# Average pooling, 2x2: one more whole store queued behind the last loads, and the last tile in two pieces instead of four

## The chip, the cores and the metric

The kernel runs on one core of one Trainium2 chip. The metric is the time of one execution on the device in microseconds (us).

## The reference

```python
# x: (32, 128, 256, 256) float32, kernel_size = 2, stride = 2; output (32, 128, 128, 128) float32
window = x[:, :, 2*i : 2*i + 2, 2*j : 2*j + 2]
output[:, :, i, j] = np.mean(window, axis=(2, 3))
```

The input is 1073.7 MB and the output 268.4 MB. Every byte is moved once.

## The kernel before

The rows of the image are taken in pairs. A unit is 128 row pairs, one on each partition: 2 KB of input and 512 B of output per partition. There are 4096 units: 127 whole tiles of 32 units (numbers 0 to 126) and a last tile of 32 units that goes in pieces. A whole tile is a load of 8.39 MB (64 KB per partition) and a store of 2.10 MB (16 KB per partition).

There are two input buffers (`ins`) and three result buffers (`res`). Whole tiles alternate between buffers 0 and 1; the last tile has `res[2]`. SP (SyncE) issues the loads, DVE (VectorE) makes the sums (rows, then neighbours), ACT (ScalarE) multiplies by 0.25 and issues the stores. A load or store is a DMA: the issuing engine puts it on its queue and goes on, 16 DMA engines move it, and it has landed when it has added 16 to its semaphore. In the code, `take(engine, sem, n)` makes an engine wait until a semaphore holds n, and takes n off it.

```python
    whole, rest = divmod(units - 1, TILE)      # 127, and rest + 1 = 32
    rest += 1
    parts, a = [], 0
    while a < rest:                            # pieces of 16, 8, 4, 4 units
        b = rest if rest - a <= 4 else a + (rest - a) // 2
        parts.append((a, b, sem(f"part{len(parts)}")))
        a = b
    # ... cut: load(), scale() ...
    def sums(it, dst):
        dve.tensor_add(out=it[:, :, 0:w], in0=it[:, :, 0:w], in1=it[:, :, w:]).then_inc(halfway)
        take(dve, halfway)
        dve.tensor_add(out=dst, in0=it[:, :, 0:w:2], in1=it[:, :, 1:w:2]).then_inc(summed)

    def tile_sums(b):
        take(dve, stored[b], 16)               # the result buffer must be free again
        take(dve, loaded[b], 16)
        sums(ins[b], res[b])

    def scale_store(t, b, landed):
        take(act, summed)
        act.sem_inc(free[b])
        scale(res[b])
        take(act, scaled)
        act.dma_start(out=ot[t], in_=res[b]).then_inc(landed, 16)
    # ... cut: SP loads tiles 0 to 126 as input buffers come free ...
        take(sp, free[whole % 2])
        it, dst = ins[whole % 2], res[2]
        for a, b, part in parts:               # loads of the last tile
            sp.dma_start(out=it[:, a:b], in_=block((whole * TILE + a) * P, b - a)[0]).then_inc(part, 16)
        take(sp, held)                         # tile 126 scaled: its store goes on SP's queue
        sp.dma_start(out=ot[whole - 1], in_=res[(whole - 1) % 2]).then_inc(tail, 16)
    # ... cut: DVE sums tiles 0 to 126, then the pieces; ACT scales and stores tiles 0 to 124 ...
        for t in range(1 + 2 * pairs, whole - 1):      # only t = 125
            scale_store(t, t % 2, stored[t % 2] if t < whole - 2 else tail)
        take(act, summed)
        scale(res[(whole - 1) % 2], held)
        for a, b, _ in parts:
            take(act, summed)
            scale(dst[:, a:b])
            take(act, scaled)
            act.dma_start(out=block((whole * TILE + a) * P, b - a)[1], in_=dst[:, a:b]).then_inc(tail, 16)
```

Of the kernel before, what the change touches and what calls it, by code (L numbers as in the profile page):

```python
# [9 lines left out]
@with_exitstack  # L10
def kernel(
    ctx: ExitStack,
    tc: tile.TileContext,
    x: bass.AP,
    kernel_size: bass.AP,
    stride: bass.AP,
    out: bass.AP,
):
    nc = tc.nc
    P = nc.NUM_PARTITIONS  # L20

    n, c, h, w = x.shape
    k = int(kernel_size)
    s = int(stride)
    h_out = (h - k) // s + 1
    w_out = (w - k) // s + 1
    R = n * c * h_out
    units = R // P if R % P == 0 else 0


    if k == 2 and s == 2 and h % 2 == 0 and w == 256 and units >= 1024:
        _pool_2x2(ctx, tc, x, out, units)
    else:
        _generic_pool(ctx, tc, x, out, k, s, n, c, h, w, h_out, w_out)
# [5 lines left out]
def _pool_2x2(ctx, tc, x, out, units):  # L40
    nc = tc.nc
    P = nc.NUM_PARTITIONS
    f32 = mybir.dt.float32
    w = x.shape[3]
    w_out = w // 2
    sp, act, dve = nc.sync, nc.scalar, nc.vector

    xv = x.rearrange("n c (ho a) w -> (n c ho) (a w)", a=2)
    ov = out.rearrange("n c ho wo -> (n c ho) wo")


    in_pool = ctx.enter_context(tc.tile_pool(name="inp", bufs=2))
    out_pool = ctx.enter_context(tc.tile_pool(name="outp", bufs=3))
    ins = [in_pool.tile([P, TILE, 2 * w], f32, name="in_tile") for _ in range(2)]
    res = [out_pool.tile([P, TILE, w_out], f32, name="res") for _ in range(3)]

    def sem(name):
        return ctx.enter_context(nc.semaphore(name))

    loaded, free, stored = [[sem(f"{n}{b}") for b in range(2)] for n in ("loaded", "free", "stored")]  # L60
    halfway, summed, scaled, held, tail = [sem(n) for n in ("halfway", "summed", "scaled", "held", "tail")]



    def take(engine, sem, n=1):
        engine.wait_ge(sem, n)
        engine.sem_inc(sem, -n)  # L67

    def block(r0, g):
        rows = slice(r0, r0 + g * P)  # L70
        return xv[rows].rearrange("(p g) f -> p g f", p=P), ov[rows].rearrange("(p g) f -> p g f", p=P)

    whole, rest = divmod(units - 1, TILE)
    rest += 1
    xt = xv[0:whole * TILE * P].rearrange("(t p g) f -> t p g f", p=P, g=TILE)
    ot = ov[0:whole * TILE * P].rearrange("(t p g) f -> t p g f", p=P, g=TILE)
    parts, a = [], 0
    while a < rest:
        b = rest if rest - a <= 4 else a + (rest - a) // 2
        parts.append((a, b, sem(f"part{len(parts)}")))  # L80
        a = b

    def load(t, b):
        sp.dma_start(out=ins[b], in_=xt[t]).then_inc(loaded[b], 16)
# [7 lines that stand above are left out]
        take(dve, stored[b], 16)  # L92
        take(dve, loaded[b], 16)
        sums(ins[b], res[b])

    def scale(dst, done=scaled):
        act.mul(out=dst, in_=dst, mul=0.25).then_inc(done)  # L97
# [8 lines that stand above are left out]
    with tc.tile_critical():  # L106

        load(0, 0)
        load(1, 1)
        pairs = (whole - 2) // 2  # L110
        with sp.Fori(2, 2 + 2 * pairs, 2) as i:
            for b in range(2):
                take(sp, free[b])
                load(i + b, b)
        for t in range(2 + 2 * pairs, whole):
            take(sp, free[t % 2])
            load(t, t % 2)



        take(sp, free[whole % 2])
        it, dst = ins[whole % 2], res[2]
        for a, b, part in parts:
            sp.dma_start(out=it[:, a:b], in_=block((whole * TILE + a) * P, b - a)[0]).then_inc(part, 16)
        take(sp, held)
        sp.dma_start(out=ot[whole - 1], in_=res[(whole - 1) % 2]).then_inc(tail, 16)


        for b in range(2):
            dve.sem_inc(stored[b], 16)  # L130
        with dve.Fori(0, whole // 2):
            for b in range(2):
                tile_sums(b)
        if whole % 2:
            tile_sums(0)
        for a, b, part in parts:
            take(dve, part, 16)
            sums(it[:, a:b], dst[:, a:b])


        scale_store(0, 0, stored[0])
        pairs = (whole - 3) // 2
        with act.Fori(1, 1 + 2 * pairs, 2) as i:
            for b in (1, 0):
                scale_store(i + 1 - b, b, stored[b])
        for t in range(1 + 2 * pairs, whole - 1):
            scale_store(t, t % 2, stored[t % 2] if t < whole - 2 else tail)
        take(act, summed)
        scale(res[(whole - 1) % 2], held)
        for a, b, _ in parts:  # L150
            take(act, summed)
            scale(dst[:, a:b])
            take(act, scaled)
            act.dma_start(out=block((whole * TILE + a) * P, b - a)[1], in_=dst[:, a:b]).then_inc(tail, 16)


        take(sp, tail, 16 * (len(parts) + 2))
# [95 lines left out]
```

## Time and profile before

| | before |
|---|---|
| median of 3 runs | 3103.59 us (3103.52 to 3103.79) |
| profiled span | 3101.5 us |
| moved by DMA | 1342.19 MB at a mean of 433 GB/s |
| DVE, ACT busy | 54%, 15% |

The head of the page of before: busy time by engine (us, share of the span), then the span in 40 slices, where a digit is tenths of busy time.

```profile
DVE 1679.6 (54%) x262; ACT 464.7 (15%) x132; POOL 0.2 (0%) x4
...
DMA  9999999999999999999999999999999999999999
...
DMA packets 37728, 1342.19 MB, mean 433 GB/s; under 512 B 4192, under 2 KB 4192, under 8 KB 4576
```

The DMA is full from end to end and neither compute engine is near its limit, so the kernel is bound by its bytes. The Trainium skill, "DMA: Bandwidth & Descriptors", section Where 436 GB/s comes from, puts the ceiling of the fabric on the side of SBUF, the on-chip memory, at 435 GB/s. The trace agrees: from 500 to 1500 us it moved 434 GB/s. (The same section expects transfers between HBM, the main memory, and SBUF, as these are, to be bound by HBM at about 358 GB/s; the measurement decides.) Only the first and last microseconds can be made better.

The tail is therefore what matters. The timeline of before: start, duration, engine, line, operation, and in brackets the idle time ahead of it.

```profile
3033.88 0.34 SPq L84 DMA_DIRECT2D in_tile<-in_x_dram  x1
3037.71 0.34 ACTq L104 DMA_DIRECT2D out_dram<-res  x1
...
3058.06 1.84 SPq L124 DMA_DIRECT2D in_tile<-in_x_dram  x4
3061.76 0.35 ACTq L104 DMA_DIRECT2D out_dram<-res  x1
3067.57 8.69 DVE L87 TENSOR_TENSOR in_tile<-in_tile 128x8192 f32<-128x8192 f32 x1 [9.71 <-DVEq L67]
3076.41 4.43 DVE L89 TENSOR_TENSOR res<-in_tile 128x4096 f32<-128x4096 f32 x1
3080.75 4.42 DVE L87 TENSOR_TENSOR in_tile<-in_tile 128x4096 f32<-128x4096 f32 x1
...
3084.66 0.35 SPq L126 DMA_DIRECT2D out_dram<-res  x1
...
3094.44 0.69 DVE L89 TENSOR_TENSOR res<-in_tile 128x512 f32<-128x512 f32 x1
3095.25 0.63 ACT L97 ACTIVATE res<-res 128x512 f32<-128x512 f32 x1 [1.34 <-ACTq L67]
3095.98 0.34 ACTq L154 DMA_DIRECT2D out_dram<-res  x1
```

The lines are, in order: the load of tile 126, the store of tile 124, the four loads of the last tile, the store of tile 125 (here on the ACT queue), the sums of tile 126, the first sum of the last tile, the store of tile 126, and the end of the last piece. DVE works from 3067.57 to 3095.13 without a gap worth naming.

The trace also gives the time from issue to landing. The load of tile 126 took 31.6 us (landed 3065.5). The store of tile 124 took 29.6 us (landed 3067.3), just before DVE started. The store of tile 125 took 19.5 us (landed 3081.3), and the last store, of 0.26 MB, 4.4 us (landed 3100.4). The line of the last store, with its size and the time to landing:

```profile
out_dram<-res ACTq DMA_DIRECT2D x1, 256.0 KB, 4.4
```

The fine windows of before: stretch, its length, busy time of DVE, ACT and POOL, clock, share of the 16 DMA engines, GB/s. A packet, the piece in which a DMA engine moves data, counts in full in the stretch in which it starts, so a share can exceed 1.

```profile
3098.50:3098.75 0.25, 0.00 (x0) 0.00 (x0) 0.00 (x0) 1.00 1.00 385
3098.75:3099.00 0.25, 0.00 (x0) 0.00 (x0) 0.00 (x0) 1.00 0.38 139
3099.00:3099.25 0.25, 0.00 (x0) 0.00 (x0) 0.00 (x0) 1.00 0.11 41
...
3099.75:3100.00 0.25, 0.00 (x0) 0.00 (x0) 0.00 (x0) 1.00 0.04 16
3100.00:3100.25 0.25, 0.00 (x0) 0.00 (x0) 0.00 (x0) 1.00 0.00 0
```

The DMA is full until about 3098.8.

### The profile page before, as it was taken

To read this page: it belongs to the slowest core of one execution; us is meant where nothing else is said; L and a number is where in the kernel's file an instruction comes from. 1 tells how busy PE (TensorE), PEld (TensorE's weight loads), DVE (VectorE), ACT (ScalarE), POOL (GpSimd) and SP (SyncE) were. 2 spreads that over 40 slices of the span, in tenths; PEclk is the share of its full clock that TensorE was granted. 3 is DMA by queue.
4 is the path that set the end of the run, shared out by engine and by line. 5 is a ranking of instruction groups with operands and counts; after the bars stand their busy time and mean duration, and the time that the engine had idled before them with its cause. 6 is when DMAs were issued, how large, how long until landed. Compare 5 with 4: busy or idle time off the path is not lost. (4 is left out here: it accounts for less than half of the span.)

```text
span 3101.5 us, 2614 instructions
## 1 busy us (share of the span) xinstructions
DVE 1679.6 (54%) x262; ACT 464.7 (15%) x132; POOL 0.2 (0%) x4
## 2 busy tenths in 40 slices
DVE  4555555555555555555555555555555555555556
ACT  1111111111111111111111111111111111111111
POOL 0000000000000000000000000000000000000000
DMA  9999999999999999999999999999999999999999
GB/s 416 436 440 426 436 440 426 437 440 424 438 440 423 439 437 425 440 428 434 440 433 430 442 423 436 439 427 440 435 426 437 439 427 436 438 424 439 437 425 416
DMA packets 37728, 1342.19 MB, mean 433 GB/s; under 512 B 4192, under 2 KB 4192, under 8 KB 4576
## 3 DMA queue, kind: packets, MB, share of 16 engines
q1 hardware_dynamic: 19008, 1075.85, 80.1%
q10 hardware_dynamic: 18720, 266.35, 20.1%
HBM read 1073.74 MB, written 268.44 MB: 433 GB/s over the span
## 5 line engine op out<-in xcount | busy, mean ns | idle before, releaser
L87 DVE TENSOR_TENSOR in_tile<-in_tile 128x8192 f32<-128x8192 f32 (+1 forms) x131 | 1113.0, 8496 | 1396.4 <-DVEq L67 1396.4
L97 ACT ACTIVATE res<-res 128x4096 f32<-128x4096 f32 (+1 forms) x131 | 463.5, 3538 | 2594.8 <-ACTq L67 2594.8
L89 DVE TENSOR_TENSOR res<-in_tile 128x4096 f32<-128x4096 f32 (+1 forms) x131 | 566.8, 4327 | 19.2
L97 ACT ACT_TABLE_LOAD x1 | 1.3, 1283 | 36.3 <-ACTq L67 36.3
L234 POOL MEMSET const-bfloat16-1.0<- 128x1 bf16 x1 | 0.1, 101 | 0.0
L234 POOL MEMSET const-uint8-127<- 128x1 uint8 x1 | 0.1, 101 | 0.0
L234 POOL MEMSET const-float32-0.0<- 128x1 f32 x1 | 0.1, 98 | 0.2 <-issue 0.2
L234 POOL MEMSET const-float32-1.0<- 128x1 f32 x1 | 0.1, 98 | 0.0
## 6 DMA issues: line engine op xcount, KB each, us to landing
out_dram<-res ACTq DMA_DIRECT2D x126, 2048.0 KB, 30.8
in_tile<-in_x_dram SPq DMA_DIRECT2D x1, 4096.0 KB, 22.0
in_tile<-in_x_dram SPq DMA_DIRECT2D x1, 2048.0 KB, 27.1
in_tile<-in_x_dram SPq DMA_DIRECT2D x2, 1024.0 KB, 30.0
out_dram<-res SPq DMA_DIRECT2D x1, 2048.0 KB, 11.7
in_tile<-in_x_dram SPq DMA_DIRECT2D x127, 31.5
out_dram<-res ACTq DMA_DIRECT2D x1, 1024.0 KB, 8.1
out_dram<-res ACTq DMA_DIRECT2D x1, 512.0 KB, 6.0
```

The lines of the kernel that those rows point to most:

```text
L87: dve.tensor_add(out=it[:, :, 0:w], in0=it[:, :, 0:w], in1=it[:, :, w:]).then_inc(halfway)
L89: dve.tensor_add(out=dst, in0=it[:, :, 0:w:2], in1=it[:, :, 1:w:2]).then_inc(summed)
L97: act.mul(out=dst, in_=dst, mul=0.25).then_inc(done)
L234: nc = _bacc.Bacc("TRN2", target_bir_lowering=False, num_devices=1)
```

## The change

Its intent is to let the last loads pass first, since sums and stores hang on them, and to fill the DMA afterwards with stores that are ready. The store of tile 125 moves from the ACT queue to the SP queue, where it stands behind the last loads, as the store of tile 126 already did. The last tile goes in two halves of 16 units instead of pieces of 16, 8, 4 and 4.

```diff
-        b = rest if rest - a <= 4 else a + (rest - a) // 2
+        b = rest if a else (rest + 1) // 2
 # ... cut: the semaphore held becomes held[0], held[1] ...
-        take(sp, held)
-        sp.dma_start(out=ot[whole - 1], in_=res[(whole - 1) % 2]).then_inc(tail, 16)
+        for k, t in enumerate((whole - 2, whole - 1)):
+            take(sp, held[k])
+            sp.dma_start(out=ot[t], in_=res[t % 2]).then_inc(tail, 16)
 # ... cut ...
-        for t in range(1 + 2 * pairs, whole - 1):
-            scale_store(t, t % 2, stored[t % 2] if t < whole - 2 else tail)
-        take(act, summed)
-        scale(res[(whole - 1) % 2], held)
+        for t in range(1 + 2 * pairs, whole - 2):
+            scale_store(t, t % 2, stored[t % 2])
+        for k, t in enumerate((whole - 2, whole - 1)):
+            take(act, summed)
+            if k == 0:
+                act.sem_inc(free[t % 2])
+            scale(res[t % 2], held[k])
```

More of the change, by code (lines that the diff above doesn't have):

```diff
@@ L60, in _pool_2x2 @@
     loaded, free, stored = [[sem(f"{n}{b}") for b in range(2)] for n in ("loaded", "free", "stored")]
-    halfway, summed, scaled, held, tail = [sem(n) for n in ("halfway", "summed", "scaled", "held", "tail")]
+    halfway, summed, scaled, tail = [sem(n) for n in ("halfway", "summed", "scaled", "tail")]
+    held = [sem(f"held{k}") for k in range(2)]
     def take(engine, sem, n=1):
```

## The prediction

> **What bounds the kernel now.** The DMA engines. The page's head gives a span of 3101.5 us in which 1342.2 MB move at a mean of 433 GB/s; the slices show DMA at 9 tenths everywhere; DVE is 54%, ACT 15% busy. The Trainium skill ("DMA: Bandwidth & Descriptors", Where 436 GB/s comes from) puts the ceiling at 435 GB/s; the trace agrees: loads alone at the start (second tile's sums begin 19.3 us after the first's, for 8.39 MB) run at 434 GB/s, like the mixture in the middle. Only the ends are elastic. In fine windows DMA is full until about 3098.9; the last store lands at 3100.4 (issued 3095.98, 4.4 us to landing).
>
> **The tail before, from the timeline.** DVE starts tile 126 at 3067.57, when the store of tile 124 (issued 3037.71, 29.6 us) lands, not when its load does (3033.88 + 31.6 = 3065.5). From there DVE works almost gapless to 3095.13: whole tile to 3080.84, the half of 16 units 3080.75 to 3087.61, then 8, 4 and 4 units. The part loads land at 3080.1, 3085.6, about 3088.1 and 3090; the store of tile 125 competes with them and lands at 3081.3.
>
> **What the change does.** No byte is added or removed. The 2.10 MB store of tile 125 moves from the ACT queue, where it shares engines with the last loads, to the SP queue behind them (the skill, same page, Queues, rings and completion order: a ring is consumed in order, engines round-robin between rings). Estimate: 2.10 MB / 434 GB/s = 4.8 us, so the last load lands near 3085.4 instead of 3090. The last tile goes in 2 pieces instead of 4.
>
> **On the critical path.** The earlier loads are worth almost nothing: DVE is occupied with tile 126 until 3080.8 and the first half until 3087.6 in both versions, and the second half is there by then. The end changes. Second half: DVE 3087.53 + 4.42 + 0.15 + 2.29 = 3094.4 (0.7 us earlier than now); ACT 1.91 us instead of 0.63, so the last store is issued at about 3096.5 instead of 3096.0; and it is 1.05 MB instead of 0.26. After 3096.5 only 0.98 MB moved before, so the DMA must run out of other stores first: a gap of about 0.2 us plus 0.6 us from issue to first byte. Then 1.05 MB / 434 = 2.4 us: data end near 3099.5 to 3099.9, landing near 3101.2. Net: **+0.8 us**.
>
> **Predicted time: 3104.4 us, 8 in 10 between 3102.6 and 3106.8.** Chances: faster by over 2%: 0.003; within 2%: 0.994; slower by over 2%: 0.003. A tail change cannot move 62 us.
>
> **What would show each step.** (a) The two part loads land near 3076 and 3085 us. (b) Sums of tile 126 still start near 3067.6, the chain of DVE stays gapless, ends near 3094.4. (c) The stores of tiles 125 and 126 on the SP queue land near 3090 and 3096. (d) The last store is issued near 3096.5 and takes 4.5 to 5 us to land; fine windows show a DMA dip around 3096 to 3097.5. (e) Middle unchanged, about 434 GB/s.
>
> **What would make it wrong.** If the SP queue with two stores behind loads drains less evenly over the 16 engines, the tail grows by a few us. If the deferred stores leave the DMA with backlog at 3096.5, the last store shares with them and ends 1 us later still. A drift of 0.1% in the middle is 3 us and hides everything.

## The result, and the profile after

| | before | after |
|---|---|---|
| median of 6 runs each | 3103.60 us (3103.26 to 3103.79) | 3103.68 us (3102.89 to 3104.79) |
| ratio of the fast runs | | 1.0001, 95% interval 0.9988 to 1.0014 |
| profiled span | 3101.5 us | 3101.1 us |

The interval is about 4 us to either side. A difference in the tail of less than that has to be read from the traces.

For that I count from one event that the change does not touch: the issue of the load of tile 126, at 3033.88 us in before and 3033.53 us in after. The 0.35 us between the two arose earlier in the run and is not the change's.

The timeline of after, for the same stretch; its line numbers are a few higher.

```profile
3033.53 0.34 SPq L85 DMA_DIRECT2D in_tile<-in_x_dram  x1
3037.38 0.34 ACTq L105 DMA_DIRECT2D out_dram<-res  x1
...
3057.73 0.86 SPq L125 DMA_DIRECT2D in_tile<-in_x_dram  x2
3061.42 23.25 SPq L128 DMA_DIRECT2D out_dram<-res  x2
3067.23 8.69 DVE L88 TENSOR_TENSOR in_tile<-in_tile 128x8192 f32<-128x8192 f32 x1 [9.71 <-DVEq L68]
3076.07 4.42 DVE L90 TENSOR_TENSOR res<-in_tile 128x4096 f32<-128x4096 f32 x1
3080.42 4.42 DVE L88 TENSOR_TENSOR in_tile<-in_tile 128x4096 f32<-128x4096 f32 x1
...
3087.19 4.42 DVE L88 TENSOR_TENSOR in_tile<-in_tile 128x4096 f32<-128x4096 f32 x1
...
3091.76 2.29 DVE L90 TENSOR_TENSOR res<-in_tile 128x2048 f32<-128x2048 f32 x1
3094.17 1.91 ACT L98 ACTIVATE res<-res 128x2048 f32<-128x2048 f32 x1 [4.86 <-ACTq L68]
3096.19 0.35 ACTq L159 DMA_DIRECT2D out_dram<-res  x1
```

The two halves landed 17.8 and 27.1 us after their issue, at about 3075.5 and 3085.2 us. In before the last three loads had landed at 3085.6 and later, up to about 3090.5. So the loads did come earlier, as intended. DVE took no notice: it started tile 126 at the same distance from the reference event (33.70 us in after, 33.69 us in before), again had no gap, and took up the second half at 3087.19, two microseconds after that half had landed.

The fine windows of after, in the columns used above.

```profile
3096.00:3096.25 0.25, 0.00 (x0) 0.08 (x1) 0.00 (x0) 1.00 1.08 459
3096.25:3096.50 0.25, 0.00 (x0) 0.00 (x0) 0.00 (x0) 1.00 0.40 164
3096.50:3096.75 0.25, 0.00 (x0) 0.00 (x0) 0.00 (x0) 1.00 0.09 33
3096.75:3097.00 0.25, 0.00 (x0) 0.00 (x0) 0.00 (x0) 1.00 0.00 0
3097.00:3097.25 0.25, 0.00 (x0) 0.00 (x0) 0.00 (x0) 1.00 1.26 524
...
3099.25:3099.50 0.25, 0.00 (x0) 0.00 (x0) 0.00 (x0) 1.00 1.26 524
3099.50:3099.75 0.25, 0.00 (x0) 0.00 (x0) 0.00 (x0) 1.00 0.04 0
```

There is now a hole between 3096.25 and 3097.00. The stores that were held back are done, and the last store (1.05 MB) has just been issued at 3096.19. The idle shares add up to 0.60 + 0.91 + 1.00 quarters, 0.63 us. But the end is sharp: the last packets end within 0.14 us of each other, the last at 3099.70, where in before one or two engines trailed for a microsecond. The last store landed 3.9 us after its issue, at 3100.1:

```profile
out_dram<-res ACTq DMA_DIRECT2D x1, 1024.0 KB, 3.9
```

Counted from the reference event that is 66.5 us, as in before. The last store was issued 0.56 us later than in before (62.66 us after the reference event against 62.10) and took 0.57 us less to land (3.86 against 4.43, from the landing times that the traces keep). That the two cancel is an accident of the sizes.

### The profile page after: what moved, and what is told of

Read it like the earlier page. It is cut to its first block, busy times and chain, and to the rows that moved or that the text cites. A ratio compares the mean times of both kernels' runs of the same rounds, so it can differ in the third digit from the quotient of the medians.

```text
span 3101.1 us, 2596 instructions
## 1 busy us (share of the span) xinstructions
DVE 1679.2 (54%) x258; ACT 464.5 (15%) x130; POOL 0.2 (0%) x4
## 5 line engine op out<-in xcount | busy, mean ns | idle before, releaser
L88 DVE TENSOR_TENSOR in_tile<-in_tile 128x8192 f32<-128x8192 f32 x129 | 1112.8, 8626 | 1396.0 <-DVEq L68 1396.0
L98 ACT ACTIVATE res<-res 128x4096 f32<-128x4096 f32 x129 | 463.2, 3591 | 2595.1 <-ACTq L68 2595.1
L90 DVE TENSOR_TENSOR res<-in_tile 128x4096 f32<-128x4096 f32 x129 | 566.6, 4392 | 18.9
## 6 DMA issues: line engine op xcount, KB each, us to landing
out_dram<-res ACTq DMA_DIRECT2D x125, 2048.0 KB, 30.8
```

What stands on the lines that cost most here:

```text
L98: act.mul(out=dst, in_=dst, mul=0.25).then_inc(done)
```

## The experiments

Theory T: the end of the run is set by the later of two things. One is the DMA's backlog, which has a floor because the bytes are fixed. The other is the chain from the last load over sums, scale and store. The rivals are named in the expectations. Except for the two large cases, the differences are too small for the times, so I also give for each run the distance from the issue of tile 126's load to the last landing, taken from the times that its trace keeps. There is one profiled run of each kernel (two of after, 0.02 us apart), so I do not read differences of 0.1 us.

| kernel | median us (range) | before, same rounds | ratio (95%) | to last landing |
|---|---|---|---|---|
| before | | | | 66.5 us |
| after | 3103.68 (3102.89 to 3104.79) | 3103.60 | 1.0001 (0.9988 to 1.0014) | 66.5 us |
| after_again | 3103.69 (3103.24 to 3104.53) | 3103.60 | 1.0000 (0.9986 to 1.0014) | 66.5 us |
| halves_only | 3106.55 (3106.30 to 3106.64) | 3103.59 | 1.0009 (0.9996 to 1.0023) | 69.5 us |
| stores_only | 3103.72 (3102.84 to 3104.03) | 3103.59 | 0.9999 (0.9986 to 1.0013) | 66.6 us |
| third_buffer | 3103.37 (3103.14 to 3103.98) | 3103.59 | 0.9999 (0.9986 to 1.0013) | 66.3 us |
| third_four | 3104.02 (3103.12 to 3105.30) | 3103.60 | 1.0001 (0.9988 to 1.0015) | 66.6 us |
| uneven | 3103.92 (3103.77 to 3105.25) | 3103.60 | 1.0002 (0.9988 to 1.0016) | 66.9 us |
| one_piece | 3112.00 (3111.99 to 3112.11) | 3103.59 | 1.0027 (1.0013 to 1.0041) | 75.1 us |

All were correct. Each had 5 rounds; after, from the result above, has 6 runs.

### halves_only: the two halves without the held-back store

```diff
 # in the kernel before
-        b = rest if rest - a <= 4 else a + (rest - a) // 2
+        b = rest if a else (rest + 1) // 2
```

> The kernel before with the last tile in two halves, both stores left where they were (tile 125 on the ACT queue). Theory T (the tail is set by whichever is later of the DMA's backlog and the chain last load, sums, scale, store; deferring the store is what lets the second half land before DVE is free): the second half lands near 3090 us as the last part did before, DVE idles about 2.5 us for it, the last store is issued near 3099.1 and lands 3.9 us later, near 3103.0: +2.6 us on the kernel before. Rival R1 (deferring the store brings nothing, the two edits are independent and each neutral): within 0.5 us of before.

Measured: 3.0 us slower than before by the medians, 2.9 us by the distance to the last landing. None of the 5 runs came within 1.9 us of before's slowest. (The interval of the ratio touches 1, as it does for any difference below about 4 us.) The timeline of halves_only:

```profile
3090.59 4.42 DVE L87 TENSOR_TENSOR in_tile<-in_tile 128x4096 f32<-128x4096 f32 x1 [2.87 <-DVEq L67]
3095.16 2.29 DVE L89 TENSOR_TENSOR res<-in_tile 128x2048 f32<-128x2048 f32 x1
3097.58 1.91 ACT L97 ACTIVATE res<-res 128x2048 f32<-128x2048 f32 x1 [7.82 <-ACTq L67]
3099.60 0.34 ACTq L154 DMA_DIRECT2D out_dram<-res  x1
```

DVE waits 2.87 us for the second half, a wait that after does not have. R1 falls: the two edits are not independent. Half of the change alone is a loss, and the other half just pays for it.

This run also shows the last store on an empty DMA: the fine windows have nothing from 3097.5 on, the first bytes in the quarter from 3100.25, and the landing came 3.9 us after the issue. So the 3.9 us in after is the plain cost of a store of 1.05 MB: the end of after is set by the chain that leads to the last store, and not by a backlog.

### stores_only: the held-back store without the two halves

```diff
 # in the kernel after
-        b = rest if a else (rest + 1) // 2
+        b = rest if rest - a <= 4 else a + (rest - a) // 2
```

> The kernel after with the old four parts (16, 8, 4, 4 units); both stores behind the loads. T: loads land about 5 us earlier (last part near 3085.3) but DVE is gapless with or without that, ends near 3095.1, last store issued 3096.0, lands near 3100.4: within 0.3 us of before. R1: the same. A rival R2 (earlier loads are worth their 4.8 us): 2 us or more faster.

Measured: 3103.72 us, 0.1 us above before. The pieces of 8, 4 and 4 units landed 22 to 26 us after their issue instead of 27 to 31, almost 5 us earlier. The last store was issued 62.12 us after the reference event, against 62.10 before. R2 falls: 5 us on the loads were worth nothing, because DVE was still occupied.

### third_buffer: does DVE's chain set the end?

DVE's start on tile 126 waits for the store of tile 124 to free its result buffer. Here tile 126 takes the third result buffer, which is free, and the last tile takes the buffer of tile 124 later.

```diff
 # in the kernel after
-        it, dst = ins[whole % 2], res[2]
+        it, dst = ins[whole % 2], res[0]
-            sp.dma_start(out=ot[t], in_=res[t % 2]).then_inc(tail, 16)
+            sp.dma_start(out=ot[t], in_=res[2 if k else 1]).then_inc(tail, 16)
-            tile_sums(0)
+            take(dve, loaded[0], 16)
+            sums(ins[0], res[2])
+            take(dve, stored[0], 16)
-            scale(res[t % 2], held[k])
+            scale(res[2 if k else 1], held[k])
```

> The kernel after, with tile 126 summed into the third result buffer, so it does not wait for the store of tile 124; the last tile takes the buffer of tile 124. T (DMA floor): DVE starts tile 126 about 2 us earlier (with its load, near 3065.5), the last store is issued near 3094.4 with backlog still there, the dip in the DMA is gone, the data end at the floor of about 3098.6 to 3098.9: only 0.4 to 0.7 us faster than after. Rival R3 (the DVE chain sets the end): the whole 2.0 us faster.

Measured: 3103.37 us; to the last landing 66.3 us, 0.2 us less than after. The timeline of third_buffer, whose load of tile 126 was issued at 3034.17:

```profile
3065.93 8.69 DVE L88 TENSOR_TENSOR in_tile<-in_tile 128x8192 f32<-128x8192 f32 x1 [7.78 <-DVEq L68]
...
3094.96 0.35 ACTq L161 DMA_DIRECT2D out_dram<-res  x1
```

DVE started 31.76 us after the reference event instead of 33.70, that is with the landing of the load; so it was the store of tile 124 that had held it. The last store was issued 60.79 us after the event instead of 62.66, 1.9 us earlier. And it landed only 0.2 us earlier, because its time to landing grew from 3.9 to 5.5 us. The fine windows of third_buffer show where it waited:

```profile
3096.50:3097.00 0.50, 0.00 (x0) 0.00 (x0) 0.00 (x0) 1.00 0.97 410
...
3098.00:3098.50 0.50, 0.00 (x0) 0.00 (x0) 0.00 (x0) 1.00 1.04 442
3098.50:3099.00 0.50, 0.00 (x0) 0.00 (x0) 0.00 (x0) 1.00 0.55 229
3099.00:3099.50 0.50, 0.00 (x0) 0.00 (x0) 0.00 (x0) 1.00 0.08 33
```

The hole is gone, the DMA is full until about 3098.8, and the ragged end is back. R3 falls: 1.9 us of the chain bought 0.2 us. T is upheld in kind; the gain I expected (0.4 to 0.7 us) was two to three times too large.

### one_piece: the last tile whole

```diff
 # in the kernel after
-        b = rest if a else (rest + 1) // 2
+        b = rest
```

> The kernel after with the last tile in one piece of 32 units: the suspected cost (last store on an empty DMA, whole chain behind the last load) made large. T: load lands near 3085.4, DVE 13.3 us to 3098.9, ACT 3.6 us, store of 2.10 MB issued near 3102.8 on an empty DMA, 3.9 + 2.4 = 6.3 us to landing, near 3109: +8.6 us on before. R4 (the DMA's total is all that counts and the pieces do not matter): within 1 us of before.

Measured: 3112.00 us, 8.4 us above before. DVE waits 3.57 us for the load, starts at 3085.77, and the store of 2.10 MB is issued at 3102.88, 68.8 us after the reference event, on a DMA that has been idle since about 3095. It lands 6.3 us later. R4 falls: when nothing is left to overlap with, the pieces count.

With halves_only this gives the cost of a store on an empty DMA. 1.05 MB took 3.9 us and 2.10 MB took 6.3 us. The second 1.05 MB cost 2.4 us (437 GB/s, or 433 from the unrounded times), which leaves 1.5 us of fixed cost. This is a fit through two points. The packets of after itself show 0.85 us from the issue to the first packet (the same within 0.02 us in halves_only and one_piece), 2.66 us of packets (about 395 GB/s) and 0.35 us from the last packet to the landing.

### after_again, third_four and uneven: the floor, and the spread

after_again is the kernel after, unchanged.

> The kernel after, unchanged, once more: its six first runs spread over 1.9 us, before's over 0.5. If the spread comes from the change (uneven drain of the stores behind the loads), it is again over 1.5 us and differs from before's of the same rounds; if it is noise of the session, 1 us or less. Median within 0.4 us of before. In the trace the dip of the DMA ahead of the last store is again there and the last store takes 3.9 us to land.

Measured: the spread was 1.3 us, before's of the same rounds 1.5 us. That is between the two limits I had set, but before's is as large, so the wider spread of the first runs is not the change's. The hole and the 3.9 us were there again. The hole (3096.5 to 3097.75) was about twice as long, 1.2 us of the DMA, and still the last store landed 66.5 us after the reference event. So in this kernel the length of the hole does not set the end; the issue of the last store and its 3.9 us do.

third_four is third_buffer with the pieces 16, 8, 4, 4.

```diff
 # in third_buffer
-        b = rest if a else (rest + 1) // 2
+        b = rest if rest - a <= 4 else a + (rest - a) // 2
```

> Tile 126 into the third result buffer and the four old parts, both stores behind the loads. T (floor of the DMA's bytes): the chain is about 1.7 us earlier and the last store is a quarter of the size, and still the data end at the same distance (about 65.0 us) after the issue of tile 126's load: within 0.3 us of third_buffer, which had 66.3 us from that issue to the last landing. Rival R5 (a small last store and an early chain still buy time): 0.5 us or more below third_buffer.

Measured: 66.6 us to the last landing, 0.3 us above third_buffer, so at the edge of what T allows and on the wrong side for R5. The last store was issued at 3094.42, 60.2 us after the reference event and earlier than in any other kernel. It held 0.26 MB and took 6.4 us to land. Chain and last store were both at their best, and nothing was gained. R5 falls. With the same pieces stores_only issued its last store 1.9 us later and also ended at 66.6 us: with four pieces it is the backlog that sets the end. Why this floor lies 0.3 us above that of third_buffer was not tested.

uneven has pieces of 24 and 8 units.

```diff
 # in the kernel after
-        b = rest if a else (rest + 1) // 2
+        b = rest if a else 3 * rest // 4
```

> The kernel after with pieces of 24 and 8 units. T: the load of 24 units lands near 3080.3 us, just as DVE is free; the store of 24 units is issued near 3093.4, when the stores of tiles 125 and 126 are almost drained, the last one (0.52 MB) near 3095.4 with backlog: no dip ahead of the last store, data end near 3099.0: 0.1 to 0.4 us faster than after, too little for the times alone.

Measured: 66.9 us to the last landing, 0.4 us worse than after and not better, so this expectation missed. The DMA had no dip ahead of the last store, as expected, but the hole had only moved ahead of the store of 24 units: in the half microseconds from 3093.5 to 3095.0 the DMA's share is 0.09, 0.08 and 0.00, about 1.5 us lost in all. That store was issued at 3094.55, 0.64 us later than expected (counted from the reference event), when the held-back stores had all but drained. It and the store of 8 units, together 2.10 MB, took 6.4 us to land from there, close to the 6.3 us of the one store of 2.10 MB on an empty DMA in one_piece. So the chain was late. Most of that is its start: DVE started tile 126 at 34.28 us after the reference event instead of 33.70, because the store of tile 124 took 30.2 us to land instead of 29.6.

The traces show a likely reason. The next two fences are the DMA view of before, by queue (packets, MB, share of the engines): first in the steady part, 3010 to 3030 us, then while the first half (32 KB per partition) loads beside the store of tile 125, 3067 to 3075 us.

```profile
q1 hardware_dynamic: 113, 6.36, 73.3%
q10 hardware_dynamic: 113, 1.59, 18.6%
```

```profile
q1 hardware_dynamic: 72, 2.36, 68.2%
q10 hardware_dynamic: 76, 1.25, 36.3%
```

q1 is the SP queue with the loads, q10 the ACT queue with the stores. In both stretches the packets alternate about one to one. With 64 KB of load to a packet and 16 KB of store, loads get four times the bytes; with 32 KB, about twice. If what the trace calls a packet is one of the page's, this agrees with the Trainium skill, "DMA: Bandwidth & Descriptors", Queues, rings and completion order, which says that an engine takes turns between queues by the packet. The store of tile 124 landed after 29.6 us with a first piece of 16 units, 30.2 us with 24 and 30.8 us with 32: the smaller the load's pieces, the more of the DMA goes to a store beside them. The three kernels (after, uneven, one_piece) differ in the pieces alone, so that the size acts is shown. That it acts through the packets' turns is argued from the counts.

The same stretch of after, 3067 to 3075 us, shows the change's first edit directly: the stores are not there.

```profile
q1 hardware_dynamic: 126, 3.64, 105.3%
```

## Why the prediction was right

**What bounds the kernel.** Right. The middle ran at 434 GB/s in both kernels (500 to 1500 us). A kernel with everything earlier (third_four) did not end earlier.

**The loads come earlier and this is worth almost nothing.** Right. The halves landed at 3075.5 and 3085.2 us against 3076 and 3085 predicted. stores_only shows the 5 us on the loads to be worth nothing by themselves. halves_only shows what I had not said: they are needed for the other edit, which without them costs 3.0 us.

**DVE's chain.** Right. It starts when the store of tile 124 has landed (third_buffer moved the start by removing that wait), has no gap, and ended at 3094.05 us, which is 3094.4 on before's clock, as predicted.

**The held-back stores.** Right: they landed near 3090.1 and 3095.9 us against 3090 and 3096.

**The hole and the last store.** The hole was there, between 3096.25 and 3097.05 (predicted: a dip around 3096 to 3097.5), and the store was issued at 3096.19, which is 3096.5 on before's clock, as predicted. (One term of the hole, a latency that no trace of this case shows, is cut from the prediction above. Measured, the first packet came 0.85 us after the issue.) The mis-sized term is the store's time to landing: 4.5 to 5 us predicted, 3.9 measured. I had added to the end of the data the distance from "DMA is full until about 3098.9" to the landing at 3100.4 in before, 1.5 us. But the data of before did not end at 3098.9: one or two engines worked on until 3099.95, and the landing followed within 0.5 us. The store of after, alone on an empty DMA, ended on all engines within 0.14 us and landed 0.35 us after the last packet. Its data themselves took a little longer than predicted, 2.66 us against 2.4. So the +0.8 us came out as nothing, 66.5 us to the last landing in both. The prediction also did not say why the two ends should lie so close, and there is no rule behind it: the end of after is set by the chain, with the last store on an empty DMA, while with four pieces the end is set by the backlog (stores_only and third_four).

**The time.** 3104.4 us was predicted with a range of 3102.6 to 3106.8; the median was 3103.68. Before's own 3103.60 us lies in that range too, so the time alone does not test the account; the steps above do. The sign of the predicted 0.8 us is neither shown nor refuted by the times; the traces of after and after_again show no such loss.

Where did the intended gain go? It had at most about 1 us to win: the gap between the DMA's last full moment and its last byte. The earlier loads found DVE occupied; what remained was spent on a larger last store behind a hole. None of the versions tried beats before by more than the noise. third_buffer is 0.2 us below it by the medians, inside the spread.

## What to carry to other kernels

When the DMA is full to the end, reordering loads and stores in the tail moves no bytes; look first at how long the DMA is not full near the end, because that is all there is to win. Splitting the last tile and ordering its transfers belong together: fewer pieces need the last load earlier, and the last store should be issued while others still fill the DMA. A store's time to landing is mostly queueing: 0.26 MB took 6.4 us behind a backlog and 1.05 MB took 3.9 us on an empty DMA.

## What the Trainium skill lacked or had wrong

- "DMA: Bandwidth & Descriptors", Anatomy of one DMA — SWDGE (gpsimd) path, gives a fit for DMAs issued from GpSimd of 2.0 us plus bytes over 436 GB/s, and none for the SP and ACT queues. Here stores from the ACT queue on an empty DMA took 1.5 us plus bytes over 437 GB/s (1.05 MB in 3.9 us, 2.10 MB in 6.3 us; a fit through two points).
- The same page, Queues, rings and completion order, says that an engine takes turns by the packet, but not what follows for a mixture: the sizes of the packets set the shares. Here packets alternated 113 to 113 and 72 to 76, so a store of 16 KB rows got about a fifth of the bytes beside loads of 64 KB rows and about a third beside 32 KB rows.
- No page gives a size for how far apart the 16 engines end. Here, behind a backlog of several stores, one or two engines worked about 1.2 us longer than the rest (before, third_buffer), while a single store on an empty DMA ended on all engines within 0.14 us (after). What makes the end ragged was not tested.
- "DMA: Bandwidth & Descriptors", Where 436 GB/s comes from, has transfers between HBM and SBUF bound by HBM at about 358 GB/s. "HBM Reference", Specifications (TRN2), has about 425 GB/s for a core that streams alone. Here one core moved 434 GB/s, loads and stores mixed.
